# Adding up the squares of an rms norm before the matrix of ones: fewer one-column products, more adds on GpSimd and VectorE

## The chip, the cores and the metric

The kernel runs on one core of one Trainium2 chip. Its engines are named as the profile names them: PE (TensorE products), PEld (TensorE weight loads), DVE (VectorE), ACT (ScalarE), POOL (GpSimd) and SP (SyncE, which issues the transfers). The metric is the device time of one execution, in microseconds; less is better.

## The reference, cut to what matters

The reference is a transformer of two parts in float32, for 256 tokens of 1024 features. Everything that the change touches is the rms norm over the features:

```
def rms_norm(x, g):
    xf = x.astype(F32)
    y = xf * lax.rsqrt(jnp.mean(xf * xf, axis=-1, keepdims=True) + EPS)
    return (y * g.astype(F32)).astype(x.dtype)

# first part: two layers
x = x + diff_attention_mixer(rms_norm(x, ...), mem, ...)      # layer A; the memory is normed too
x = x + dense_swiglu(rms_norm(x, ...), ...)
x = x + hgrn2_mixer(rms_norm(x, ...), mem, ...)               # layer B
x = x + moe_swiglu(rms_norm(x, ...), ...)                     # 8 experts, 2 for each token
x = rms_norm(x, final_norm)
# second part: twice
a = rms_norm_2(h, pre_mix_g[i])
mix = ... attention and gating of a ... @ w_o[i]
h = h + rms_norm_2(mix, post_mix_g[i])
f = conv_ffn(rms_norm_2(h, pre_ffn_g[i]), ...)
h = h + rms_norm_2(f, post_ffn_g[i])
gate = sigmoid(rms_norm_2(h, ple_norm_g[i]) @ w_ple_gate[i])
h = h + gate * (p[i] @ w_ple_proj[i])
```

That makes sixteen norms over 1024 features in one execution.

## The kernel before, in words

Activations are kept transposed: features on the 128 partitions, tokens along the free dimension. x is `xr`, eight blocks of 128 features by 256 tokens; `xpair(i)` is two such blocks side by side, 128x512. Products go into PSUM tiles of 128x512; each float32 operand is split into a rounded high part and a rest, and a product is made of three (`mm3`, L258 to L260, operands by features; `mm3t`, L264 to L266, by tokens). Weights are loaded by SP in pieces of 1 MB and split by ACT (L229, high part) and DVE (L230, rest).

A norm is never applied to the operand: the products are made with x itself, and what comes out is multiplied by 1/rms. So the work of a norm runs beside the products that need it. It has these steps.

1. `squares` (L333 to L340): ACT squares the four pairs of x into four tiles `sq` of 128x512 (L334). With `how="later"` POOL adds the second to the first and the fourth to the third (L337), and two tiles are left. Otherwise DVE adds the second and the third to the first (L339), and the first and the fourth are left.
2. `stats_r` (L342 to L355): PE sums over the partitions, by products that have a 128x128 block of `sq` as weights and the column `onec` (all 1/1024) as the moving operand (L350). The two tiles make eight such products into `ms`, one column for each 128 tokens; each stands in the trace as two records. DVE adds EPS (L353, tile `s`), POOL takes the power -1/2 (L354, tile `r`).
3. `rows_R` (L357 to L366): PE transposes `r` into `R`, 1/rms along the free dimension (L361), and DVE copies it to SBUF in most places (L365).

Eleven norms are of the kind "later": those of layer A and of its memory, of the dense block, of layer B, of the mixture of experts, and in each of the two rounds of the second part one before the mixer, one before the feed-forward block and one before the gate. Five are of the other kinds: `final_norm` (how="now") and the four in `post` (how="acc"), which norm a sum `acc` that lies in PSUM after its last product. In these five everything that follows needs the result: the products of the next block have the normed x as operand. `fill` gives PE part of another product there (`proj`, tiles `pj`); by the numbers in FILL it does so in `final_norm` and in the two `post` of the second round, and not in the two `post` of the first.

The code writes a norm ahead of the products of its block. Where its instructions stand on each engine is settled when the program is built: they are placed among the instructions that are written behind them, and from then on each engine takes its instructions in that order. PE's order is what matters below: a product on `sq` that is not ready holds up all products behind it.

Of the kernel before, what the change touches and what calls it, by code (L numbers as in the profile page):

```python
# [15 lines left out]
OP = mybir.AluOpType  # L16
# [77 lines left out]

# vectors over the features, as columns of 128: (key, how many columns)
COLS = [("a_norm_mix", 8), ("a_mem_norm", 8), ("b_mem_norm", 8), ("dense_norm", 8), ("b_norm_mix", 8), ("moe_norm", 8),
# [14 lines left out]
def layout(v):  # L111
    """the arrays of the launch: the weights as they come, the rest laid out as the chip reads it"""
    def feat(a):
        n = a.shape[1] // 128
        return a.T.reshape(n, 128, a.shape[0]).transpose(1, 0, 2)

    arr = {k: v[k] for k in WEIGHTS}
    arr["consts"] = CONSTS
    arr["xt"] = feat(v["x"][0])
    arr["memt"] = feat(v["mem"][0])  # L120
    router = v["moe_router"][0].reshape(8, 128, 8).transpose(1, 0, 2).reshape(128, 64)
    arr["cols"] = np.concatenate([v[k].reshape(n, 128).T for k, n in COLS] + [router], 1)
    arr["cols2"] = np.stack([np.concatenate(
        [v[k][i].reshape(n, 128).T for k, n in COLS_2]
        + [v["cmp_w2_2"][i].reshape(2, 2, 128, 64).transpose(2, 0, 1, 3).reshape(128, 256)], 1) for i in range(2)])
    arr["rows"] = np.concatenate([v[k].reshape(-1) for k, _ in ROWS]
                                 + [v[k][i].reshape(-1) for i in range(2) for k, _ in ROWS_2])
    arr["pt"] = np.stack([feat(v["p_2"][i, 0]) for i in range(2)])
    arr["wst"] = v["gmlp_ws_2"].transpose(0, 3, 1, 2).reshape(2, 128, 1024)
    return {k: np.ascontiguousarray(a) for k, a in arr.items()}  # L130
# [3 lines left out]
def body(ctx: ExitStack, tc: tile.TileContext, I, out, stop=None):  # L134
# [53 lines left out]
    def C(n, dt=F32):  # L188
        """n columns that stay"""
        o = used[dt]  # L190
        used[dt] += n
        assert used[dt] <= keep[dt].shape[1]
        return keep[dt][:, o:o + n]
# [52 lines left out]
    def wpieces(w, k0, kn, c0, width, s):  # L246
        """wtile in pieces of 512, which leaves its tiles to what is under way"""
        wh, wl = Pieces(), Pieces()
        for k in range(kn):
            for f in range(width // 512):  # L250
                st, hi, lo = G("st" + s), G2("hi" + s, F32R), G("lo" + s, F32R)
                nc.sync.dma_start(st, w[(k0 + k) * 128:(k0 + k) * 128 + 128, c0 + f * 512:c0 + f * 512 + 512])
                split(st, hi, lo, None)
                wh.tiles[k, f], wl.tiles[k, f] = hi, lo
        return wh, wl
# [67 lines left out]
    def sumsq(dst, src, n, eng):  # L323
# [3 lines left out]
        else:  # L327
            V.scalar_tensor_tensor(j[:, :n], src, 1.0 / n, src, op0=OP.mult, op1=OP.mult, accum_out=dst)

    def squares(src, how):  # L330
        """tiles whose sum over features, through the matrix of ones, is the mean square"""
        sq = [J("sq") for _ in range(4)]
        for i in range(4):  # L333
            A.activation(sq[i], src(i), AF.Square)  # L334
            if how == "later":
                if i % 2:
                    GP.tensor_tensor(sq[i - 1], sq[i - 1], sq[i], op=OP.add)  # L337
            elif i in (1, 2):
                V.tensor_tensor(sq[0], sq[0], sq[i], op=OP.add)  # L339
        return sq[0:3:2] if how == "later" else sq[0:4:3]  # L340

    def stats_r(src, how="later"):  # L342
        """1 / rms over the 1024 features, by token"""
        tiles = squares(src, how)
        ps = PC("ms")
        for n, t in enumerate(tiles):
            for c in range(2):
                for kk in range(2):
                    o = kk * 256 + c * 128
                    T.matmul(ps[:, c:c + 1], lhsT=t[:, o:o + 128], rhs=onec, start=n == 0 and c == 0 and kk == 0,  # L350
                             stop=n == len(tiles) - 1 and kk == 1, skip_group_check=True)
        r, m = S(2, "r"), S(2)
        V.tensor_scalar(m, ps[:, 0:2], EPS, None, op0=OP.add)  # L353
        GP.tensor_tensor(r, m, neghalf[:, :2], op=OP.pow)  # L354
        return r  # L355

    def rows_R(r, keep=True):  # L357
        """the same along the free dimension"""
        pr = PC("R")
        for c in range(2):  # L360
            T.transpose(pr[:, c * 128:c * 128 + 128], r[:, c:c + 1].to_broadcast([128, 128]), ident)  # L361
        if not keep:
            return pr[:, :256]
        R = G("R")
        V.tensor_copy(R[:, :256], pr[:, :256])  # L365
        return R[:, :256]  # L366
# [40 lines left out]
    def feat_1024(X, w, s, order, side=None, hook=None):  # L407
        """X times w, by features; side yields what it makes of X while the rest is multiplied"""
        acc = acc_open()
        for n, kp in enumerate(order):  # L410
            if side is not None and n == len(order) - 1:
                steps(side)
            wh, wl = wtile(w, kp * 2, 2, 0, 1024, s)
            acc_rows(acc, wh, wl, [(X.hi(k), X.lo(k)) for k in (kp * 2, kp * 2 + 1)], n == 0, n == len(order) - 1,
                     side)
            if side is not None:
                steps(side, 1)
            if hook is not None and n == 1:
                hook()
        return acc  # L420
# [39 lines left out]

# [1 line left out]
    opening = wload(I["a_w_in"][0], 0, 8, 0, 256, "q")  # L462
# [5 lines left out]

# [1 line left out]
    def mem_load():  # L470
# [5 lines left out]
    def steps(gen, n=None):  # L476
        """runs n steps of a generator (all of them without n); whether it goes on"""
        while n is None or n > 0:
            if next(gen, 0) == 0:
                return False  # L480
            n = None if n is None else n - 1
        return True
# [37 lines left out]
    def by_R(lst, R, f=None, tile=G):  # L520
        """keeps a product by features, times R"""
        def done(ps):
# [8 lines left out]
    def by_r(lst, r, func=AF.Copy, tile=G):  # L531
        """keeps a product by tokens, times r"""
        def done(ps):
            g = tile("tk")
            for c in range(2):
                A.activation(g[:, c * 256:c * 256 + 256], ps[:, c * 256:c * 256 + 256], func, scale=r[:, c:c + 1])
            lst.append(g)
        return done
# [6 lines left out]
    def mem_attn(qmT, kmT, vm, XC):  # L545
        """attention over the memory (queries scaled), its output in pair 3 of XC"""
        cc = G("ccm")
# [43 lines left out]
    def head_rms(po, extra, XC, hp, col):  # L591
        """rms norm of two heads by token and (times extra), then their transposes, split"""
        sq = J("sq")
# [70 lines left out]

# [1 line left out]
    def layer_a():  # L666
# [115 lines left out]

# [1 line left out]
    def layer_b(kv_b, X, r, R):  # L784
# [204 lines left out]

# [1 line left out]
    def moe(acc):  # L991
        # the first weights, before the branch
        ahead = []
# [20 lines left out]
        for k in range(8):  # L1014
            for c in range(2):
                T.matmul(pl[:, c * 8:c * 8 + 8], lhsT=xr[:, k, c * 128:c * 128 + 128], rhs=wr[:, k * 8:k * 8 + 8],
                         start=k == 0 and c == 0, stop=k == 7, skip_group_check=True)
        # tokens by rows, split
        xh = [[G("xh", F32R) for _ in range(2)] for _ in range(2)]
# [45 lines left out]

        # the rms of the tokens, and the weights of their two experts
        r = stats_r(xpair)
# [147 lines left out]

# [1 line left out]
    shared, names = {}, {}  # L1217

    def prep_half(X, k, cols):
        """the operand of feature block k of x"""  # L1220
        if k % 2 == 0:
# [4 lines left out]
    def post(acc, gain, cols, fill):  # L1226
        """adds the normalized acc; the operand of the next products comes with it"""
        r = stats_r(lambda i: acc[i], "acc")
# [17 lines left out]
    def proj(i, out):  # L1246
        """p @ w_ple_proj, features by rows, halved (the gate's own half lies in tanh)"""
        for m in range(2):
# [18 lines left out]
    def gelu_gen(x, n):  # L1267
        """x (1 + tanh(...)) in place: twice the gelu"""
        sq, t = G2("gs"), G2("gt")
# [21 lines left out]
    def second(i, pj, fill, X):  # L1291
# [116 lines left out]

        # keys and values
        seg1 = []  # L1410
# [12 lines left out]
        steps(ex, PRE[0])  # L1423
        # queries, their two parts side by side
        qhl = []
# [144 lines left out]
        def cmp_attn(c):  # L1570
            """over the compressed keys: opens at[c]"""
            ps = PC("cs")
# [265 lines left out]
```

## Time and profile before

| | |
|---|---|
| time, median of 3 runs | 2308.17 us (2307.86 to 2312.56) |
| span of the profiled execution | 2313.2 us |
| PE busy | 2239.2 us (97%) |
| DVE, ACT busy | 1817.8 us (79%), 1474.7 us (64%) |
| POOL busy | 76.4 us (3%) |
| mean granted TensorE clock | 0.977 |

The profiled execution's own time is not listed apart from its span; the span stands 0.6 us above the highest of the three runs and 5.0 us above their median. The experts take about 1000 us in the middle of the span; no norm lies in them. The granted clock is 1.00 (2.4 GHz) or 0.50 (1.2 GHz).

### The profile page before, as it was taken

What the parts mean: (1) busy time and instruction counts of PE and PEld (TensorE: products, weight loads), DVE (VectorE), ACT (ScalarE), POOL (GpSimd) and SP (SyncE); (2) the same over time, 40 slices, a digit from 0 to 9 for tenths busy, and PEclk for the clock granted to TensorE, in tenths of its full rate; (3) what the DMA queues carried; (4) which work ended last, traced back from release to release, by engine and by line L of the source; (5) the groups of instructions that cost most, each with busy time, mean ns of one, the idle gap of its engine ahead of it and who ended that gap; (6) DMA issues with size and microseconds to landing.
All of it is one profiled execution on the core that took longest, in us unless ns stands there. A gap on an engine that the chain in (4) does not pass through costs nothing. (4 is left out here: it accounts for less than half of the span.)

```text
span 2313.2 us, 36939 instructions
## 1 busy us (share of the span) xinstructions
PE 2239.2 (97%) x14218; PEld 2019.2 (87%) x14218; DVE 1817.8 (79%) x2701; ACT 1474.7 (64%) x2138; POOL 76.4 (3%) x83
## 2 busy tenths in 40 slices
PE   8999999998999999999999999999999999989998
PEld 7889999997878888888888888879899998989998
DVE  6666576766888898989898989888777777867776
ACT  5554457435777777777777777777665565765554
POOL 0100001000000000000000000000000001000001
PEclk9999999998999999999999999999999999989998
DMA  8445556224999999999999999986245544525550
GB/s 288 139 137 174 195 171 204 92 78 167 359 348 335 349 353 372 338 354 351 373 350 341 349 378 350 372 299 221 74 136 193 182 147 137 186 78 183 183 178 19
DMA packets 297113, 551.23 MB, mean 238 GB/s; under 512 B 10336, under 2 KB 132064, under 8 KB 296928
## 3 DMA queue, kind: packets, MB, share of 16 engines
q1 hardware_dynamic: 296928, 548.78, 67.5%
q8 instruction: 114, 1.87, 0.3%
q14 instruction: 71, 0.58, 0.1%
HBM read 547.70 MB, written 1.05 MB: 237 GB/s over the span
## 5 line engine op out<-in xcount | busy, mean ns | idle before, releaser
L230 DVE TENSOR_TENSOR loe<-ste,hie 128x1024 fp32r<-128x1024 f32 x448 | 520.0, 1217 | 12.4 <-ACT hie L229 4.2
L229 ACT ACTIVATE hie<-ste 128x1024 fp32r<-128x1024 f32 x448 | 439.5, 1053 | 23.9 <-PE ac L260 9.9
L230 DVE TENSOR_TENSOR lod<-std,hid 128x1024 fp32r<-128x1024 f32 x224 | 264.9, 1218 | 17.1 <-ACT hid L229 15.6
L229 ACT ACTIVATE hid<-std 128x1024 fp32r<-128x1024 f32 x224 | 221.4, 1057 | 4.8 <-PE pg L265 2.3
L266 PE MATMUL pu<-loe,eh 128*128 128x512 f32 x448 | 176.7, 394 | 1.4 <-DVE loe L230 1.4
L1159 PE MATMUL y<-hid,hl 128*128 128x512 f32 x448 | 175.7, 392 | 2.0 <-DVE hl L284 2.0
L264 PE MATMUL pg<-hie,eh 128*128 128x512 f32 x448 | 175.4, 391 | 0.3 <-ACT eh L286 0.3
L266 PE MATMUL pg<-loe,eh 128*128 128x512 f32 x448 | 175.6, 392 | 0.0
L264 PE MATMUL pu<-hie,eh 128*128 128x512 f32 x448 | 174.7, 390 | 0.0
L265 PE MATMUL pg<-hie,el 128*128 128x512 f32 x448 | 174.6, 390 | 0.0
L265 PE MATMUL pu<-hie,el 128*128 128x512 f32 x448 | 174.6, 390 | 0.0
L1158 PE MATMUL y<-hid,hh 128*128 128x512 f32 x448 | 173.4, 392 | 0.7 <-ACT hh L283 0.7
L1137 ACT ACTIVATE eh<-pg,cw 128x512 f32<-128x512 f32 x56 | 38.6, 689 | 203.4 <-PE pg L266 203.4
L1160 PE MATMUL y<-lod,hh 128*128 128x512 f32 x448 | 163.4, 407 | 0.8
L258 PE MATMUL gu<-xh,hig 128*128 128x256 f32 x528 | 150.8, 286 | 3.7 <-ACT xh L286 3.7
L230 DVE TENSOR_TENSOR lou<-stu,hiu 128x1024 fp32r<-128x1024 f32 x66 | 80.4, 1220 | 91.1 <-PE gu L259 82.9
L259 PE MATMUL gu<-xh,log 128*128 128x256 f32 x528 | 150.5, 285 | 0.0
L260 PE MATMUL gu<-xl,hiu 128*128 128x256 f32 x528 | 150.5, 285 | 0.0
L258 PE MATMUL gu<-xh,hiu 128*128 128x256 f32 x528 | 150.4, 285 | 0.0
L259 PE MATMUL gu<-xh,lou 128*128 128x256 f32 x528 | 150.3, 285 | 0.0
L260 PE MATMUL gu<-xl,hig 128*128 128x256 f32 x528 | 150.1, 285 | 0.0
L258 PE MATMUL ac<-hh,hidn 128*128 128x256 f32 x528 | 149.4, 283 | 0.0
(516 smaller groups left out, 6279.5 us busy)
## 6 DMA issues: line engine op xcount, KB each, us to landing
ste<-in_moe_w_gate_up_dram SPq DMA_DIRECT2D x224, 1024.0 KB, 7.2
std<-in_moe_w_down_dram SPq DMA_DIRECT2D x112, 1024.0 KB, 5.5
stg<-in_w_up_dram SPq DMA_DIRECT2D x22, 1024.0 KB, 5.1
stu<-in_w_up_dram SPq DMA_DIRECT2D x22, 1024.0 KB, 5.1
stdn<-in_w_down_dram SPq DMA_DIRECT2D x22, 1024.0 KB, 4.8
stg<-in_dense_w_gate_up_dram SPq DMA_DIRECT2D x11, 1024.0 KB, 5.0
stu<-in_dense_w_gate_up_dram SPq DMA_DIRECT2D x11, 1024.0 KB, 5.0
stdn<-in_dense_w_down_dram SPq DMA_DIRECT2D x11, 1024.0 KB, 4.9
```

The lines of the kernel that those rows point to most:

```text
L229: A.activation(hi[:, :m], sq, AF.Copy)
L230: V.tensor_tensor(lo[:, :m], sq, hi.bitcast(F32)[:, :m], op=OP.subtract)
L258: T.matmul(o, lhsT=lh, rhs=rh, start=start, stop=False, **kw)
L259: T.matmul(o, lhsT=ll, rhs=rh, start=False, stop=False, **kw)
L260: T.matmul(o, lhsT=lh, rhs=rl, start=False, stop=stop, **kw)
L264: T.matmul(o, lhsT=xh, rhs=wh, start=start, stop=False, **kw)
L265: T.matmul(o, lhsT=xl, rhs=wh, start=False, stop=False, **kw)
L266: T.matmul(o, lhsT=xh, rhs=wl, start=False, stop=stop, **kw)
L1137: A.activation(t, pg, AF.Silu, scale=rc)
L1158: T.matmul(y[hf], lhsT=h[:, fs], rhs=a, start=opens, stop=False)
L1159: T.matmul(y[hf], lhsT=l[:, fs], rhs=a, start=False, stop=False)
L1160: T.matmul(y[hf], lhsT=h[:, fs], rhs=b, start=False, stop=ends)
```

## The change

The squares are added up further before PE sees them. With "later", POOL adds the second remaining tile to the first (128x512), and then the right half of that tile to its left half (128x256, the new function `halves`); one tile of 128x256 is left, and two products instead of eight. In the five other norms ACT squares the fourth pair in two halves, DVE adds the right half of the summed tile to its left half and the left half of the fourth pair's squares to that, and two tiles of 128x256 are left: four products instead of eight. Removed comments and text strings are left out of the diff.

```
+    def halves(t):
+        GP.tensor_tensor(t[:, :256], t[:, :256], t[:, 256:], op=OP.add)
+        return t[:, :256]
+
     def squares(src, how):
         sq = [J("sq") for _ in range(4)]
-        for i in range(4):
-            A.activation(sq[i], src(i), AF.Square)
-            if how == "later":
+        if how == "later":
+            for i in range(4):
+                A.activation(sq[i], src(i), AF.Square)
                 if i % 2:
                     GP.tensor_tensor(sq[i - 1], sq[i - 1], sq[i], op=OP.add)
-            elif i in (1, 2):
+            GP.tensor_tensor(sq[0], sq[0], sq[2], op=OP.add)
+            return [halves(sq[0])]
+        for i in range(3):
+            A.activation(sq[i], src(i), AF.Square)
+            if i:
                 V.tensor_tensor(sq[0], sq[0], sq[i], op=OP.add)
-        return sq[0:3:2] if how == "later" else sq[0:4:3]
+        for kk in range(2):
+            A.activation(sq[3][:, kk * 256:kk * 256 + 256], src(3)[:, kk * 256:kk * 256 + 256], AF.Square)
+        V.tensor_tensor(sq[0][:, :256], sq[0][:, :256], sq[0][:, 256:], op=OP.add)
+        V.tensor_tensor(sq[0][:, :256], sq[0][:, :256], sq[3][:, :256], op=OP.add)
+        return [sq[0][:, :256], sq[3][:, 256:]]

     def stats_r(src, how="later"):
         tiles = squares(src, how)
         ps = PC("ms")
         for n, t in enumerate(tiles):
             for c in range(2):
-                for kk in range(2):
-                    o = kk * 256 + c * 128
-                    T.matmul(ps[:, c:c + 1], lhsT=t[:, o:o + 128], rhs=onec, start=n == 0 and c == 0 and kk == 0,
-                             stop=n == len(tiles) - 1 and kk == 1, skip_group_check=True)
+                T.matmul(ps[:, c:c + 1], lhsT=t[:, c * 128:c * 128 + 128], rhs=onec, start=n == 0 and c == 0,
+                         stop=n == len(tiles) - 1, skip_group_check=True)
```

The lines behind it move down by eleven: the products `ms` are L361 after the change, the transposes L372.

**DVE in the `post` behind the first feed-forward block of the second part.** Before the change, from the two adds of squares (L339) to the step that adds EPS (L353); `lopg` are rests of the next block's weights:

```order
L339 TENSOR_TENSOR sq_32288<-sq_32288,sq_32289 128x512
L339 TENSOR_TENSOR sq_32288<-sq_32288,sq_32290 128x512
L230 TENSOR_TENSOR lopg_32525<-stpg_32522,hipg_32524 128x1024
L230 TENSOR_TENSOR lopg_32529<-stpg_32522,hipg_32528 128x1024
L353 TENSOR_SCALAR s_32308<-ms_32298 128x2
L1241 TENSOR_TENSOR pt_32311<-pt_32311,R_32323 128x256 x2
L1242 TENSOR_TENSOR keep<-keep,pt_32311 128x256 x2
```

After the change (the two new adds are L351 and L352):

```order
L348 TENSOR_TENSOR sq_32258<-sq_32258,sq_32259 128x512
L348 TENSOR_TENSOR sq_32258<-sq_32258,sq_32260 128x512
L230 TENSOR_TENSOR lopg_32490<-stpg_32487,hipg_32489 128x1024
L351 TENSOR_TENSOR sq_32258<-sq_32258 128x256
L230 TENSOR_TENSOR lopg_32494<-stpg_32487,hipg_32493 128x1024
L352 TENSOR_TENSOR sq_32258<-sq_32258,sq_32261 128x256
L364 TENSOR_SCALAR s_32277<-ms_32271 128x2
L1252 TENSOR_TENSOR pt_32280<-pt_32280,R_32292 128x256 x2
```

One split of weights now stands between the second add and the first new one, and another between the two new ones. The same holds in the three other `post`; in `final_norm` two splits and a split of `proj` stand there.

**PE in the norm ahead of the first feed-forward block of the second part.** Before the change, around its second group of `ms` and its transposes `R`; `gu` are the block's products:

```order
L258 MATMUL gu_30062<-xh_30004,hig_30046 128x256
L350 MATMUL ms_30022<-keep,sq_30014 128x1 x4
L259 MATMUL gu_30062<-xh_30004,log_30047 128x256
L260 MATMUL gu_30062<-xl_30005,hig_30046 128x256
L258 MATMUL gu_30063<-xh_30004,hig_30046 128x256
L259 MATMUL gu_30063<-xh_30004,log_30047 128x256
L260 MATMUL gu_30063<-xl_30005,hig_30046 128x256
L258 MATMUL gu_30062<-xh_30004,hiu_30056 128x256
L259 MATMUL gu_30062<-xh_30004,lou_30057 128x256
L361 MATMUL R_30035<-keep,r_30031 128x128 x2
L260 MATMUL gu_30062<-xl_30005,hiu_30056 128x256
```

After the change:

```order
L258 MATMUL gu_30033<-xh_29978,hig_30016 128x256
L259 MATMUL gu_30033<-xh_29978,log_30017 128x256
L361 MATMUL ms_29998<-keep,sq_29986 128x1 x2
L260 MATMUL gu_30033<-xl_29979,hig_30016 128x256
L258 MATMUL gu_30032<-xh_29978,hiu_30026 128x256
L259 MATMUL gu_30032<-xh_29978,lou_30027 128x256
L260 MATMUL gu_30032<-xl_29979,hiu_30026 128x256
L372 MATMUL R_30005<-keep,r_30001 128x128 x2
L258 MATMUL gu_30033<-xh_29978,hiu_30026 128x256
L259 MATMUL gu_30033<-xh_29978,lou_30027 128x256
L260 MATMUL gu_30033<-xl_29979,hiu_30026 128x256
```

The first group of `ms`, 41 products ahead, is gone; the one that is left stands seven products later among the `gu` than the second group did, and `R` four products later than before.

**PE in the first norm of the second round of the second part.** Before the change, from the second group of `ms` on; `tw` are products by tokens, 128x512:

```order
L264 MATMUL tw_32704<-hiz_8382_32741,xh_32662 128x512
L265 MATMUL tw_32704<-hiz_8382_32741,xl_32663 128x512
L266 MATMUL tw_32704<-loz_8383_32742,xh_32662 128x512
L350 MATMUL ms_32686<-keep,sq_32678 128x1 x4
L264 MATMUL tw_32703<-hiz_8382_32741,xh_32662 128x512
L265 MATMUL tw_32703<-hiz_8382_32741,xl_32663 128x512
L266 MATMUL tw_32703<-loz_8383_32742,xh_32662 128x512
L264 MATMUL tw_32704<-hiz_8382_32741,xh_32662 128x512
L265 MATMUL tw_32704<-hiz_8382_32741,xl_32663 128x512
```

After the change:

```order
L266 MATMUL tw_32664<-loz_8383_32703,xh_32627 128x512
L264 MATMUL tw_32665<-hiz_8382_32702,xh_32627 128x512
L361 MATMUL ms_32653<-keep,sq_32641 128x1 x2
L265 MATMUL tw_32665<-hiz_8382_32702,xl_32628 128x512
L266 MATMUL tw_32665<-loz_8383_32703,xh_32627 128x512
L264 MATMUL tw_32664<-hiz_8384_32706,xh_32633 128x512
L265 MATMUL tw_32664<-hiz_8384_32706,xl_32634 128x512
L266 MATMUL tw_32664<-loz_8385_32707,xh_32633 128x512
```

The first group, fifteen products ahead, is gone, and the group that is left stands four products later than the second group did.

## Rows read from the trace of the kernel before

**Rows 1.** The page: busy time, share of the span and instructions of each engine

```profile
PE 2239.2 (97%) x14218; PEld 2019.2 (87%) x14218; DVE 1817.8 (79%) x2701; ACT 1474.7 (64%) x2138; POOL 76.4 (3%) x83
```

**Rows 2.** Waits of PE: waiting line, what ended it; us in total, times, longest

```profile
PE R L361 <- POOL r L354: 8.4, 8, 1.3
...
PE ms L350 <- POOL sq L337: 4.4, 5, 1.8
```

**Rows 3.** Instructions on tile sq: count, then shortest/median/longest ns, first and last start

```profile
L350 PE MATMUL ms<-keep,sq x256: 164/250/352, 13.5 to 2290.1; 128*128 128x1 f32 x128
...
L337 POOL TENSOR_TENSOR sq<-sq,sq x22: 1273/1408/2463, 11.1 to 2286.3; 128x512 f32<-128x512 f32 x22
```

**Rows 4.** Groups by line and shape, POOL: count, busy us, mean ns, idle before

```profile
L337 POOL TENSOR_TENSOR sq<-sq,sq 128x512 f32<-128x512 f32 x22 | 36.1, 1643 | 327.9 <-ACT sq L334 291.0 <-PE ac L260 13.6 <-issue 10.7
```

**Rows 5.** Timeline, post behind the first feed-forward block: start us, us

```profile
1890.07 0.69 DVE L339 TENSOR_TENSOR sq<-sq,sq 128x512 f32<-128x512 f32 x1 [0.32 <-ACT sq L334]
...
1890.68 2.35 DVE L230 TENSOR_TENSOR lopg<-stpg,hipg 128x1024 fp32r<-128x1024 f32 x2
...
1890.91 1.92 PE L350 MATMUL ms<-keep,sq 128*128 128x1 f32 x16 [0.43 <-DVE sq L339]
...
1892.95 0.15 DVE L353 TENSOR_SCALAR s<-ms 128x2 f32<-128x2 f32 x1
...
1893.93 0.43 PE L361 MATMUL R<-keep,r 128*128 128x128 f32 x2 [1.11 <-POOL r L354]
...
1896.15 0.58 PE L258 MATMUL fp<-xh,hipg 128*128 128x256 f32 x1 [1.79 <-ACT xh L286]
```

**Rows 6.** Groups by line and shape, DVE: an add of 128x256 in SBUF

```profile
L651 DVE TENSOR_TENSOR cv<-cv 128x256 f32<-128x256 f32 x44 | 18.4, 421 | 0.0
```

**Rows 7.** Timeline, norm ahead of the second part's first feed-forward block

```profile
1705.14 2.13 POOL L337 TENSOR_TENSOR sq<-sq,sq 128x512 f32<-128x512 f32 x1 [6.36 <-ACT sq L334]
...
1707.33 1.05 PE L350 MATMUL ms<-keep,sq 128*128 128x1 f32 x8 [0.62 <-POOL sq L337]
...
1709.42 0.43 PE L361 MATMUL R<-keep,r 128*128 128x128 f32 x2
```

**Rows 8.** Timelines of POOL and of PE, norm of layer B

```profile
346.23 3.91 POOL L337 TENSOR_TENSOR sq<-sq,sq 128x512 f32<-128x512 f32 x2 [191.07 <-ACT sq L334]
...
353.12 1.84 PE L350 MATMUL ms<-keep,sq 128*128 128x1 f32 x16
...
357.57 0.43 PE L361 MATMUL R<-keep,r 128*128 128x128 f32 x2 [1.07 <-POOL r L354]
```

**Rows 9.** Timeline, first norm of the second part's second round

```profile
1929.22 2.34 POOL L337 TENSOR_TENSOR sq<-sq,sq 128x512 f32<-128x512 f32 x1 [17.96 <-ACT sq L334]
...
1930.35 1.75 DVE L1748 TENSOR_TENSOR keep<-keep,sg 128x512 f32<-128x512 f32 x1
...
1931.61 1.49 PE L350 MATMUL ms<-keep,sq 128*128 128x1 f32 x8 [1.76 <-POOL sq L337]
...
1933.90 1.27 POOL L337 TENSOR_TENSOR sq<-sq,sq 128x512 f32<-128x512 f32 x1 [2.35 <-ACT sq L334]
...
1939.22 0.95 PE L350 MATMUL ms<-keep,sq 128*128 128x1 f32 x8
```

**Rows 10.** Timeline of POOL: second add in the first and the last norm

```profile
14.68 1.28 POOL L337 TENSOR_TENSOR sq<-sq,sq 128x512 f32<-128x512 f32 x1 [2.27 <-ACT sq L334]
...
2286.26 2.22 POOL L337 TENSOR_TENSOR sq<-sq,sq 128x512 f32<-128x512 f32 x1 [3.68 <-issue]
```

**Rows 11.** Stretches: length, busy us (instructions) by engine, granted clock, DMA

```profile
147.90:155.60 7.70, 5.66 (x46) 5.46 (x47) 5.67 (x8) 3.89 (x7) 3.98 (x3) 1.00 0.00 0
1894.50:1901.30 6.80, 5.15 (x24) 5.15 (x25) 6.80 (x17) 4.58 (x10) 1.34 (x1) 0.50 0.45 150
1932.10:1938.90 6.80, 6.80 (x20) 5.54 (x20) 2.11 (x4) 2.59 (x4) 1.27 (x1) 0.50 0.23 81
...
68.40:78.60 10.20, 9.31 (x44) 9.02 (x44) 3.63 (x5) 2.66 (x4) 2.59 (x2) 0.50 0.35 119
```

## The prediction, made before the changed kernel was run

> **What bounds the kernel now.** I read the page first: PE is busy 97% of the span [rows 1]. So PE is the bound nearly everywhere, and PE work that goes away is worth its full time, unless PE then only comes earlier to a wait. Next the waits of PE: two of the longest kinds lie inside the norms, 8.4 us before the transposes `R` (for POOL's power) and 4.4 us before products `ms` (for POOL's adds) [rows 2]. PE takes its products in order, so each of these stops everything behind it. Then the instructions on `sq`: 256 records of `ms`, that is 128 products in two records each, and 22 adds on POOL of 1273 to 2463 ns [rows 3], mean 1643 [rows 4]. Last the timelines of the sixteen norms, for who waits for whom in each; four of them stand in rows.
>
> **What is removed.** Sixteen records in the norm of layer B take 1.84 us from the first start to the last end [rows 8], or about 0.12 us a record when they come one behind the other. Eleven norms lose 12 records and five lose 8: 172 records, 20.6 us of PE. That is the most that the change can give by itself; what it puts in the place of the products decides.
>
> **Five norms on the path (`final_norm`, `post`).** In the `post` behind the first feed-forward block the second add of squares ends at 1890.76, and PE then has nothing but the 16 records, 1890.91 to 1892.83; the step `s` follows at 1892.95, `R` at 1893.93, and the first product of the next block at 1896.15, after 1.79 us more of idling [rows 5]. POOL is not in this chain ahead of the power. After the change DVE's order is: second add, split, add, split, add. A split is half of 2.35 us, 1.17 [rows 5]; an add of 128x256 in SBUF takes 0.42 [rows 6]. That is 2 x 1.17 + 2 x 0.42 = 3.18 us from 1890.76, to 1893.95. Only then come the products, in PE's order all eight records behind the last add: 8 x 0.12, and `s` at 1895.0 instead of 1892.95. **+2.05 us**; nothing covers it, since PE has no other work there. The other `post` of that round, by the same rows of its own, gives +1.75. In the second round PE has products `pj` meanwhile, which now run ahead of `ms`, so that only +0.45 and +0.8 are left (there `s` follows the same 3.2 us after the second add). In `final_norm` a split of `proj` stands in DVE's order too, but most of `pj` is still to be done: +1.0. Together **+6.0 us**. The squares in two halves on ACT cost nothing: both are done while DVE is in the splits.
>
> **The eleven others: a longer chain on POOL.** Two adds more stand between POOL's second add and `ms`. The 128x512 one: 1.27 at best, 2.46 at worst, 1.64 in the mean [rows 3, 4]; I take the mean, since these are the same operands on the same engine beside the same work. The 128x256 one no row shows; it has half of the elements, so between half of the shortest and half of the longest whole add, 0.64 to 1.23; I take 0.7. The chain is 2.34 us longer, between 1.91 and 3.69.
> A rule of the Trainium skill (GPSIMD Engine Reference, section 4.1, Engine selection) speaks against this: adds of two tensors belong on VectorE, GpSimd being about two times slower. The same shape takes 0.69 on DVE [rows 5] and 1.64 on POOL [rows 4], 2.4 times. With the page's factor the chain would be 2.1 longer, not 2.34, and the sum below 2.1 us smaller, 2314.8; I go by the row.
>
> For each norm I take PE's place in the new order (so many products behind the old place, at 0.12 us for one of 256 columns, 0.23 for one of 512), without the first group of `ms` and the wait before it; compare it with POOL's new end; and count the products that now stand ahead of `R` as done.
> - Layer B: POOL's second add ends at 350.14, 3 us before PE comes to `ms`, which stands where it stood; two adds more still fit in. 12 records less, `R` waits for the power as before, all of it earlier: **-1.9** [rows 8].
> - Ahead of the second part's first feed-forward block: POOL's second add ends at 1707.27, and PE already waited 0.62 for it [rows 7]. POOL is now done at 1709.7; PE, without the first group and seven products on, is there at 1706.6 and waits 3.1 us. Then half a microsecond of `ms`, `s` and the power; `R` comes at 1711.3 instead of 1709.42, with four products (0.5 us) more behind it: **+1.4**.
> - First norm of the second round: the first group, its wait of 1.76 and the 1.49 that it took are gone. The second add ends at 1935.17, the chain at 1937.55; PE is there at 1934.2 (19 products of 0.23 from 1929.85, where its old wait began) and waits 3.4. Against 1940.2 before, with four products more done: **-3.1** [rows 9].
> - The norm of the experts gives 0: there the products wait for DVE's choice of experts, not for the norm.
> - The other seven by the same working, the first and the last of them with their second add in [rows 10]: -2.1, -2.1, 0, -0.2, +1.5, +0.7, -0.2, together -2.4.
>
> Sum **-6.1 us**; with a chain of 1.91 it would be -9.5, with 3.69 it would be +6.6.
>
> **What the new waits do to the clock.** PE's waits of about 2.5 to 3.5 us before `ms` are new in four places: the dense block's norm, those ahead of both feed-forward blocks of the second part, and the one with the -3.1. In the trace the stretch around the dense norm, which holds the longest of the old waits before `R`, 1.3 us, has a granted clock of 1.00 [rows 2, 11]. Behind the wait of 1.76 us it is 0.50, the level of 1.2 GHz, for 6.8 us [rows 9, 11], and so it is behind the `post` with its waits of 1.11 and 1.79 [rows 5, 11]. While PE has work, half of such a stretch is lost: 3.4 us for 6.8. Not all of it is work, and some stretches are shorter; I take 2.2 for each, 4 x 2.2 = **+8.8 us** (from 0, if the clock stays, to 4 x 3.4 = 13.6).
>
> **Sum.** 6.0 - 6.1 + 8.8 = +8.7 us. The profiled execution would go from a span of 2313.2 to 2321.9. That span lies 5.0 us above the median of the runs, 0.2%; I add the same 8.7 to the median: **2316.9 us**.
>
> **Rivals.**
> 1. *The clock does not fall at the new waits.* For it speaks that the stretch around the dense norm held 1.00 with two waits in it [rows 11]; against it, that the waits are now twice as long. The sum is 6.0 - 6.1 = -0.1: 2308.1, no change. Chance 0.22.
> 2. *Faster: the first groups no longer break the stream.* Around the memory's norm in layer A the clock is 0.50 for 10.2 us [rows 11], behind a first group that PE had to wait for. That group goes. If the clock stays at 1.00 over the new wait there (1.2 to 1.6 us), as it does around the dense norm with 1.3, 5.1 us come back; that is the point from which it decides. With POOL's shortest adds and no new falls as in 1, the sum is 6.0 - 9.5 - 5.1 = -8.6: 2299.6. Against it: POOL's adds rarely run at their shortest beside DVE's splits. Chance 0.12.
> 3. *Slower still: POOL holds DVE.* While POOL added for 2.34 us, an add on DVE of 128x512 took 1.75 instead of 0.69 [rows 5, 9]: 1.06 us lost. The change has 22 adds more on POOL. In most places splits lie ahead in stock and cover it; if half of the 22 hold a split or an operand that PE is about to need, 11 x 1.06 = 11.7 us come on top: 2328.6. Chance 0.14.
> The same page of the Trainium skill (section 1, Specifications) says that GpSimd shares its SBUF interfaces with VectorE, which contend where an instruction reads two inputs from SBUF; by that rule 3 has its mechanism, and the trace agrees with the 1.75.
>
> **How the numbers follow.** The forecast has 0.52, its own range 2312 to 2322 (the chain from 1.91 to 2.8, each fall of the clock 1.5 to 3 us). A measurement of this kernel can tell about 0.2%, 4.6 us, from no change: 2303.6 to 2312.8. Slower: 0.52 + 0.14, less 0.04 of the forecast that ends under 2312.8: 0.62. Same: 0.22 + 0.04. Faster: 0.12. To hold the time 8 times in 10 the range takes in rival 1 and the lower part of rival 3: 2303.5 to 2325.
>
> **What the profile would show.** Right: 84 instead of 256 records of `ms`; in the four `post` DVE's last add about 3.2 us behind the second; PE waits of 2 to 3.5 us before `ms` that end with POOL's add of 128x256; new stretches at 0.50 behind them, above all ahead of both feed-forward blocks. Wrong: POOL's two new adds together under 2 us, `ms` without waits, or the clock at 1.00 after them (rival 1); DVE's adds and splits above their old durations while POOL adds (rival 3). The prediction would fall most likely by the clock, the term least supported by rows.

## The result, and the profile of the changed kernel

The changed kernel takes 2329.28 us (median of 4 runs, 2322.25 to 2332.60), the kernel before in the same sitting 2308.02 (2306.85 to 2312.56). The two medians lie 21.3 us apart; the ratio on record over all runs is 1.0079 with a 95% interval of 1.0063 to 1.0095, which is 18.2 us more on 2308.0, and this is the number used below. Forecast were 8.7 more, 2316.9, and at most 2325. The side was right, the size less than half.

The page, part 1, in the profiled execution (2330.53 us, span 2328.7):

```profile
PE 2227.5 (96%) x14046; PEld 2005.6 (86%) x14046; DVE 1831.5 (79%) x2711; ACT 1476.0 (63%) x2143; POOL 100.6 (4%) x105
```

Beside [rows 1] the 172 records are gone and PE is busy 11.7 us less, but the span is 15.5 us longer: PE stands idle 27.2 us more. The waits of PE that have to do with norms say where (waiting line, what ended it; us in total, times, longest):

```profile
PE ms L361 <- POOL sq L332: 24.3, 11, 3.8
...
PE R L372 <- POOL r L365: 10.9, 9, 2.4
...
PE ms L361 <- DVE sq L352: 6.9, 3, 3.4
```

All eleven norms that add on POOL (the later norms from here on) now make PE wait for the fold, 24.3 us against 4.4 in five places before [rows 2]. Three of the other five wait 6.9 us for VectorE's last add. The adds themselves, from the instructions on `sq` (count, shortest/median/longest ns) and the groups by line on POOL (busy us, mean ns):

```profile
L361 PE MATMUL ms<-keep,sq x84: 169/250/374, 18.5 to 2305.5; 128*128 128x1 f32 x84
...
L343 POOL TENSOR_TENSOR sq<-sq,sq x11: 1261/1322/1366, 16.3 to 2302.7; 128x512 f32<-128x512 f32 x11
L332 POOL TENSOR_TENSOR sq<-sq x11: 726/732/1593, 17.7 to 2304.1; 128x256 f32<-128x256 f32 x11
```
```profile
L342 POOL TENSOR_TENSOR sq<-sq,sq 128x512 f32<-128x512 f32 x22 | 36.7, 1670 | 321.3 <-ACT sq L340 284.6 <-PE ac L260 13.6 <-DVE xl L287 12.3
...
L343 POOL TENSOR_TENSOR sq<-sq,sq 128x512 f32<-128x512 f32 x11 | 14.4, 1313 | 0.9
L332 POOL TENSOR_TENSOR sq<-sq 128x256 f32<-128x256 f32 x11 | 10.7, 974 | 0.9
```

Third add and fold take 1.31 + 0.97 = 2.29 us in the mean; the forecast had 1.64 + 0.70 = 2.34. The chain is as long as forecast, by two errors that cancel. What it did to the clock, in stretches behind the norms (the column after POOL's count is the granted clock):

```profile
150.40:158.10 7.70, 5.14 (x31) 5.08 (x31) 6.41 (x7) 2.56 (x3) 3.12 (x4) 0.78 0.36 122
354.90:365.10 10.20, 7.79 (x42) 7.50 (x42) 6.50 (x9) 1.77 (x3) 1.62 (x1) 0.67 1.00 311
...
1716.80:1723.60 6.80, 6.73 (x30) 6.46 (x31) 2.77 (x5) 1.81 (x2) 0.72 (x2) 0.50 0.18 63
1904.50:1914.70 10.20, 6.95 (x30) 6.49 (x31) 6.55 (x20) 5.69 (x12) 0.97 (x2) 0.50 0.33 104
1952.30:1955.70 3.40, 3.40 (x10) 2.73 (x10) 1.52 (x4) 1.06 (x1) 0.80 (x2) 0.50 0.01 2
2303.90:2310.70 6.80, 4.95 (x22) 4.66 (x23) 2.41 (x4) 0.63 (x1) 2.45 (x3) 0.50 0.00 0
```

The dense norm (first row), at 1.00 before [rows 11], has fallen to 0.50 for part of its stretch. So has layer B's (second row), where the forecast saw no wait at all. The `post` behind the first feed-forward block is at 0.50 for 10.2 us instead of 6.8. The first norm of the second round (the row at 1952.30), at 0.50 for 6.8 us before [rows 11], is there for 3.4.

At ScalarE's first square of a norm, the changed kernel is 0.9 us ahead in the dense norm, then behind: 5.8 us at the experts' norm, 7.0 at the first `post`, 13.2 at the norm ahead of the gate in the first round, 14.0 in the last. One step lies around the dense and layer B norms, one around the two `post` of the first round and the norms behind them.

Layer B's norm shows both ways in which POOL's chain tells (start us, us):

```profile
347.03 4.25 POOL L342 TENSOR_TENSOR sq<-sq,sq 128x512 f32<-128x512 f32 x2 [192.12 <-ACT sq L340]
...
351.36 1.37 POOL L343 TENSOR_TENSOR sq<-sq,sq 128x512 f32<-128x512 f32 x1
351.48 2.32 DVE L230 TENSOR_TENSOR lofz<-stfz,hifz 128x1024 fp32r<-128x1024 f32 x1
352.80 1.59 POOL L332 TENSOR_TENSOR sq<-sq 128x256 f32<-128x256 f32 x1
353.73 1.34 DVE L287 SCALAR_TENSOR_TENSOR xl<-keep,xh 128x256 fp32r<-128x256 f32 x2
...
354.45 0.67 PE L361 MATMUL ms<-keep,sq 128*128 128x1 f32 x4 [1.57 <-POOL sq L332]
354.99 3.48 DVE L230 TENSOR_TENSOR lofz<-stfz,hifz 128x1024 fp32r<-128x1024 f32 x3
358.39 0.15 DVE L364 TENSOR_SCALAR s<-ms 128x2 f32<-128x2 f32 x1
358.46 1.21 DVE L230 TENSOR_TENSOR lofz<-stfz,hifz 128x1024 fp32r<-128x1024 f32 x1
358.62 1.62 POOL L365 TENSOR_TENSOR r<-s,keep 128x2 f32<-128x2 f32 x1 [4.23 <-DVE s L364]
...
360.30 0.43 PE L372 MATMUL R<-keep,r 128*128 128x128 f32 x2 [2.41 <-POOL r L365]
```

PE waits 1.57 us for the fold. And POOL and VectorE hold each other up. The split that starts 0.12 us behind POOL's third add takes 2.32 us, where the three at 354.99, with POOL idle, take 3.48 together. The fold starts while that split runs and takes 1.59 us; the split at 358.46 starts ahead of POOL's power and takes its usual 1.21, and the power takes 1.62 us. The products are done at 355.12, but `s` has to stand behind three more splits, until 358.39, and `R` waits 2.41 us where it waited 1.07 [rows 8]. Before the change `s` stood behind three splits as well, but these came 2.7 us earlier:

```profile
352.27 3.48 DVE L230 TENSOR_TENSOR lofz<-stfz,hifz 128x1024 fp32r<-128x1024 f32 x3
355.67 0.14 DVE L353 TENSOR_SCALAR s<-ms 128x2 f32<-128x2 f32 x1
```

### The profile page after: what moved, and what is told of

Its sections match the earlier page's. It is cut to its first block, busy times and chain, and to the rows that moved or that the text cites. A ratio compares the mean times of both kernels' runs of the same rounds, so it can differ in the third digit from the quotient of the medians.

```text
span 2328.7 us, 36637 instructions
## 1 busy us (share of the span) xinstructions
PE 2227.5 (96%) x14046; PEld 2005.6 (86%) x14046; DVE 1831.5 (79%) x2711; ACT 1476.0 (63%) x2143; POOL 100.6 (4%) x105
## 3 DMA queue, kind: packets, MB, share of 16 engines
q8 instruction: 112, 1.84, 0.3%
HBM read 547.70 MB, written 1.05 MB: 236 GB/s over the span
```

## The experiments

Each kernel ran beside the kernel before; the last column works the ratio out on 2308.0 us. "At 0.50" is 2 x (1 - mean granted clock) x span, in the mean over the runs: the time at the lower of the two levels that the stretches show. The kernel before has 90 to 98 us of it in the sittings.

| run | ratio, 95% interval | at 0.50, us | us |
|---|---|---|---|
| changed kernel | 1.0079 (1.0063 to 1.0095) | 128 | +18.2 |
| e1 POOL's part alone | 1.0066 (1.0053 to 1.0079) | 117 | +15.2 |
| e2 VectorE's part alone | 1.0021 (1.0010 to 1.0032) | 102 | +4.8 |
| e3 POOL's part without the fold | 1.0042 (1.0029 to 1.0055) | 109 | +9.7 |
| e4 later norms added on VectorE | 0.9872 (0.9856 to 0.9887) | 74 | -29.5 |
| e5 as e1, `ms` further back | 0.9984 (0.9975 to 0.9993) | 95 | -3.7 |
| e6 before, its pairs on VectorE | 0.9917 (0.9904 to 0.9930) | 79 | -19.2 |
| e7 before, two idle adds more on POOL | 1.0042 (1.0028 to 1.0057) | 98 | +9.7 |
| e8 before, `ms` further back | 0.9929 (0.9916 to 0.9943) | 78 | -16.4 |
| e9 changed, waits fed | 1.0054 (1.0041 to 1.0067) | 90 | +12.5 |
| e10 as e2, adds ahead of the splits | 0.9995 (0.9986 to 1.0004) | 91 | -1.2 |
| e11 e4 and e10 | 0.9871 (0.9856 to 0.9885) | 79 | -29.8 |
| e12 as e4 without the fold | 0.9880 (0.9867 to 0.9894) | 70 | -27.7 |
| e13 changed kernel again | 1.0078 (1.0065 to 1.0091) | 130 | +18.0 |
| e14 changed, waits fed to fit | 1.0054 (1.0039 to 1.0069) | 101 | +12.5 |
| e15 as e7, behind the power | 1.0024 (1.0015 to 1.0033) | 95 | +5.5 |

**Which part costs (e1 to e4).** e1 keeps the old code of the five other norms, e2 that of the later norms. e3 is e1 with:

```diff
-            return [halves(sq[0])]
+            return [sq[0]]
```

and e4 is e1 with all adds of the later norms on VectorE:

```diff
             for i in range(4):
                 A.activation(sq[i], src(i), AF.Square)
-                if i % 2:
-                    GP.tensor_tensor(sq[i - 1], sq[i - 1], sq[i], op=OP.add)
-            GP.tensor_tensor(sq[0], sq[0], sq[2], op=OP.add)
-            return [halves(sq[0])]
+                if i:
+                    V.tensor_tensor(sq[0], sq[0], sq[i], op=OP.add)
+            V.tensor_tensor(sq[0][:, :256], sq[0][:, :256], sq[0][:, 256:], op=OP.add)
+            return [sq[0][:, :256]]
```

Expected of e1: 

> Only the eleven later norms are changed (third add and fold on GpSimd, 4 records); final_norm and the four post stay as before. My theory now, by the offsets between the two traces: these norms carry about 9 of the 15.5 us by which the profiled span grew, through waits of PE before ms that end with POOL's fold and through the clock behind them: 2315 to 2320 us, ratio 1.003 to 1.005. Rival, the forecast's own terms (first groups of products gone, -6.1; clock +8.8): +2.7, 2311 us. Rival, only the five norms on the path cost: 2302 to 2308.

Expected of e2: 

> Only final_norm and the four post are changed (squares of half tiles, fold and third add on VectorE, 8 records); the eleven later norms stay as before. By the working of the forecast and by the offsets of the trace after: +6 to +6.5, 2314 to 2315 us, ratio 1.0026 to 1.0028; with a fall of the clock behind the two long waits of PE up to +9. Rival, these norms carry nearly the whole loss: 2321 to 2327.

Expected of e3: 

> The later norms with POOL's third add of 128x512 but without the fold: 4 products in 8 records from one tile; the other five norms as before. The chain on POOL is 0.7 to 1.6 us shorter than in the run with the fold, and PE has 4 records more. If the length of the chain decides (each microsecond is waited for by PE): about 5 us under the run with the fold and its waits before ms shorter by 0.7 to 1.6. If every new wait costs alike because the clock falls behind it, whatever its length: within 2 us of the run with the fold.

Expected of e4: 

> The later norms with all four adds on VectorE (three of 128x512, one fold of 128x256, as each square comes), none on GpSimd; 4 records; the other five norms as before. Theory that GpSimd's slow adds, and what they hold up on VectorE, are the loss: sums are ready some 4 us earlier, no waits of PE before ms, 2300 to 2306 us. Rival, VectorE is full around the norms (83% busy over the span) and 2.5 us of adds in each of 11 norms push splits back that PE needs: 2312 to 2325 us, with PE waiting for xl and lo instead.

The parts add up, 15.2 + 4.8 = 20.0 against 18.2, and POOL's part carries three quarters; e1 lies above its expected 1.003 to 1.005. e3 bears out the length of the chain: 5.5 us come back with the fold gone. e4 ended far below every expectation of mine (the 83% in its text is a slip; VectorE is 79% busy in both kernels): the same 4 records in each norm, the same number of adds, and 45 us less than e1. Its waits:

```profile
PE R L371 <- POOL r L364: 6.6, 8, 1.2
...
PE ms L360 <- DVE s L1056: 3.0, 1, 3.0
...
PE ms L360 <- DVE sq L348: 2.7, 2, 2.2
...
PE ms L360 <- DVE sq L343: 1.2, 1, 1.2
```

PE waits before `ms` of a later norm in two places, 4.2 us in all, against 24.2 in e1. But two things differ from e1, not one: who adds, and where `ms` stands. Where VectorE makes the adds, the order that is settled when the program is built has `ms` further back. Products that stand ahead of `ms` in PE's order, from the start of the program, those of `ms` and `R` not counted (the second group, in the kernel before):

| norm | before | changed | e4 | e5 |
|---|---|---|---|---|
| layer A, memory | 373 | 381 | 412 | 417 |
| dense | 912 | 919 | 944 | 943 |
| ahead of the first feed-forward block, second part | 13735 | 13742 | 13768 | 13768 |
| the same, second round | 16330 | 16335 | 16364 | 16366 |
| the last | 17936 | 17950 | 17969 | 17966 |

**Place or engine (e5 to e8).** e5 is e1, and e8 the kernel before, with the products of `ms` traced at a lower priority, one number for each later norm, which moves them to where e4 has them in eight of the eleven (not in the first norm, layer B's and the experts'):

```diff
+    LATE = [400, 132, 74, 0, 0, 78, 154, 95, 86, 152, 126]
...
+        with tc.high_priority(-LATE.pop(0) if how == "later" else 0):
```

e6 is the kernel before with `V.tensor_tensor` for `GP.tensor_tensor` in the two adds. e7 is the kernel before with, in each later norm, an add of 128x512 and one of 128x256 more on POOL, on squares that nobody reads any more.

Expected of e5: 

> As the run of GpSimd's part alone (its chain of four adds, 4 records in each later norm), but the products ms stand further back in TensorE's order in eight of the eleven norms: 10 to 40 products later, where they stand when VectorE makes the adds. Theory of the place: the loss came from products that stood too early for GpSimd's chain; with 1.2 to 4 us of other products ahead of them PE no longer waits, about 19 us of idling and the clock behind it come back and most of the way to the run with VectorE's adds is made: 2285 to 2300 us. Rival, the engine: GpSimd's adds hold VectorE's splits up by about 10 us more than before, wherever ms stands, and the wait goes to xl, lo or R: 2312 to 2325 us.

Expected of e6: 

> The kernel before with its two adds of each later norm on VectorE instead of GpSimd; 16 records as before, no add more. Theory of the engine (GpSimd's adds are long, vary and hold VectorE): most of the 29 us that VectorE's adds gave come without any record less: 2285 to 2298 us. Theory of the count: the 132 records fewer carry it (15.8 us of PE), so here only some 5 to 10 us: 2299 to 2305. Theory of the place: the second group stands 5 to 11 products further back only, about 5 to 8 us: 2301 to 2306.

Expected of e7: 

> The kernel before, with two adds more on GpSimd in each later norm (128x512 and 128x256, on squares that are no longer needed) behind the power, where nobody waits for them: the price of GpSimd's adds for the work beside them alone. If what they hold up on VectorE (excess over usual durations 10.8 us in the trace before, 20.7 in the changed one) reaches the path: 5 to 12 us more, 2315 to 2322. If VectorE's stock of splits covers it: within 3 us of the kernel before.

Expected of e8: 

> The kernel before (two adds on GpSimd, 16 records), only its products ms stand further back in TensorE's order in the later norms, both groups together where they stand when VectorE makes the adds. Theory of the place: the waits for the first groups (0.99, 0.79 and 1.76 us in the trace before) and the stretches of half clock behind them go: 8 to 18 us less, 2293 to 2303 us. If the place is worth nothing without the fewer records and the free VectorE: 2307 to 2313.

Both theories hold in part: e6 and e7 ended as that of the engine had it, e8 as that of the place, and e5 between the two. The place of `ms` is worth 18.9 us in e5 against e1, and 16.4 in e8 against the kernel before, where nothing else is changed. With `ms` at its new place in both, POOL's longer chain costs 12.7 us (e5 against e8) although it saves 132 records. e5 still waits for the fold in six norms:

```profile
PE ms L363 <- POOL sq L332: 13.1, 6, 3.0
...
PE R L374 <- POOL r L367: 10.6, 7, 3.7
```

e6 gains 19.2 us with 16 records as before, but it does not show the engine alone: in its order the first groups of `ms` stand up to 30 products further back too, and the second up to 11, which its expectation left out for the first. With the place held, e4 against e5 shows the engine: the same four adds and 4 records, `ms` within five products of the same place in ten of the eleven norms, and 25.8 us between them. In e7 two adds that nobody reads cost 9.7 us. They stood ahead of the power in POOL's order in most norms, though, so that I tried them again behind it:

```diff
+            for add in (GP.tensor_tensor(a, a, c, op=OP.add),
+                        GP.tensor_tensor(c[:, :256], a[:, :256], a[:, 256:], op=OP.add)):
+                tc.add_manual_dep(add.ins, power.ins.name, ...)
```

Expected: 

> The kernel before with the two extra adds on GpSimd in each later norm strictly behind the power, so that nothing on GpSimd waits for them; TensorE's order is that of the kernel before. What is left of the 9.7 us of the earlier run is VectorE held up alone. If that was the price: 5 to 10 us more than before, 2317 to 2321. If the delay of the power was: within 3 us of the kernel before.

5.5 us remain, between the two expectations. They may be VectorE held up, or tiles of squares that come free later since POOL still reads them; the runs don't separate these.

**VectorE's part (e10 to e12).** In e10 the splits that stood between the adds of the five other norms are ordered behind the last add; e11 puts e10 and e4 together; e12 is e4 without the fold.

Expected of e10: 

> As the run of VectorE's part alone (final_norm and the four post changed), but in each of these five norms the two splits of weights that stood between the second, the third and the fourth add come behind the fourth. The term of the forecast for these norms was 2 x 1.17 us of splits plus two adds of 0.42, less the records that go. If the splits in between are the price: the sum is there 2.3 us earlier in each, the loss of about 5 us goes, 2306 to 2311 us. Rival, the splits are then late themselves by 0.84 us and the next block waits for them, or the two adds and ScalarE's half squares are the price: 2313 to 2317.

Expected of e11: 

> Both that helped or may help: the later norms with all four adds on VectorE and 4 records, and the five other norms changed as in the run with the adds ahead of the splits (8 records). If the parts add up: the 2281 us of the first, changed by what the other run of this call shows against the kernel before, between -3 and +3: 2278 to 2285 us, under both kernels. If VectorE's adds in the one delay the splits of the other: 2285 to 2292.

Expected of e12: 

> The later norms with three adds on VectorE and no fold: 4 products in 8 records, standing 8 to 13 products earlier in TensorE's order than with the fold. Two adds on VectorE with 16 records gave 0.9917 of the time before, four adds with 4 records 0.9872. If the count of records carries that difference, each 44 of them (12 us per 100): 0.988 to 0.990, 2284 to 2288 us. If the place in TensorE's order carries it: nearer to the run with two adds, 2288 to 2292; if the fold on VectorE costs more than its 4 records: 2277 to 2281.

e10: the loss of e2 is gone, so the splits in between were its price. The same place, the `post` behind the first feed-forward block, in the changed kernel and then in e10 (timelines of DVE and PE):

```profile
1901.15 0.69 DVE L348 TENSOR_TENSOR sq<-sq,sq 128x512 f32<-128x512 f32 x1 [0.32 <-ACT sq L346]
...
1902.90 0.42 DVE L351 TENSOR_TENSOR sq<-sq 128x256 f32<-128x256 f32 x1
1903.23 1.22 DVE L230 TENSOR_TENSOR lopg<-stpg,hipg 128x1024 fp32r<-128x1024 f32 x1
1904.37 0.42 DVE L352 TENSOR_TENSOR sq<-sq,sq 128x256 f32<-128x256 f32 x1
...
1904.93 1.84 PE L361 MATMUL ms<-keep,sq 128*128 128x1 f32 x8 [3.37 <-DVE sq L352]
...
1906.81 0.16 DVE L364 TENSOR_SCALAR s<-ms 128x2 f32<-128x2 f32 x1 [2.02 <-PE ms L361]
```
```profile
1890.38 0.69 DVE L353 TENSOR_TENSOR sq<-sq,sq 128x512 f32<-128x512 f32 x1 [0.32 <-ACT sq L351]
1891.11 0.42 DVE L356 TENSOR_TENSOR sq<-sq 128x256 f32<-128x256 f32 x1
1891.83 0.43 DVE L357 TENSOR_TENSOR sq<-sq,sq 128x256 f32<-128x256 f32 x1 [0.30 <-ACT sq L355]
...
1892.40 1.02 PE L370 MATMUL ms<-keep,sq 128*128 128x1 f32 x8 [1.62 <-DVE sq L357]
...
1893.46 0.16 DVE L373 TENSOR_SCALAR s<-ms 128x2 f32<-128x2 f32 x1
```

From the second add to `s` it is 5.66 us in the one, 3.08 in the other. But 8 records fewer bring nothing either: e10 is no faster than the kernel before, and e11 no faster than e4. e12 against e6 and e4: going from 16 records to 8 on VectorE gives 8.5 us, from 8 to 4 another 1.8, less than the intervals can tell; in both steps `ms` moves back as well, so that these are no prices of the records alone.

**The clock (e9, e13, e14).** In the changed kernel, products of 128x256 whose result is not used stand right ahead of `ms` in each later norm, on squares that are ready after POOL's second add: four in e9, one to three in e14, by the wait. They fill the wait with work; `ms` itself stands within seven products of its place in the changed kernel.

Expected of e9: 

> The changed kernel with four products of 128x256 more in each later norm, right ahead of ms in TensorE's order (on squares that are there after GpSimd's second add; their result is not used). They run in the wait for the third add and the fold and bring ms no earlier. Over the runs so far the mean granted clock gives about 92 us of half clock before and 128 after, and the span without half of that is the same in both, 2263 us. Theory that the clock is the loss: the falls go although the chain is as long, half clock back to 95 to 110 us, 2312 to 2321 us. Rival, the waits themselves are the loss: 2328 to 2334 us, the feeding products costing a little more where a wait is short.

Expected of e13: 

> The changed kernel once more, on the chip of the two other runs of this call: 1.0063 to 1.0095 of the time before, half clock by the mean granted clock of the runs 120 to 136 us.

Expected of e14: 

> The changed kernel with one to three feeding products in each later norm instead of four, as many as its wait before ms holds by the trace of the changed kernel. If the clock makes 12 to 18 of the 18 us: half clock near 90 to 100 us as with four, less delay of R, 2312 to 2319 us. If the falls cost little and the waits are the loss: half clock may rise again, 2322 to 2330 us.

The time at 0.50 falls from 130 us (e13) to 101 (e14) and 90 (e9, the level of the kernel before), with a chain on POOL as long as ever. The total gains 5.5 us by the ratios of e13 and e14 (7.5 by their medians, 2328.14 and 2320.67), and the intervals just touch: e9, 2320.5 by its ratio, lies at the upper edge of what the theory of the clock expected, and e14, with the same total, between its two theories. The feeding products are in the way themselves: e14's 27 are 54 records, and PE now waits longer for `R`.

```profile
PE R L388 <- POOL r L381: 14.8, 13, 4.0
...
PE ms L374 <- POOL sq L332: 5.7, 8, 1.3
```

So the falls do come from PE's idling before `ms`, and 5.5 us is the least that they seem to cost. How much they cost in all I can only estimate. In the 68 runs of the kernel before in the four sittings of the experiments, the time at 0.50 goes from 78 to 106 us, and the span rises 0.36 us for each of it; where PE works all through, it would be half a microsecond, since 0.50 is half of 1.00. The 36 to 39 us more of the changed kernel are then 13 to 20 us. The slope need not be the clock's alone: longer waits in a run would raise both.

## Why the prediction was too low

- *172 records, 20.6 us*: the count is right, 84 are left. That they are worth 0.12 us each on the path no run shows: from e6 to e4 132 of them go for 10.3 us, with two more adds on VectorE and `ms` further back, and in e10 the 40 of the other five norms bring no gain clear of the noise.
- *Five norms on the path, +6.0*: right. e2 gives 4.8 (2.3 to 7.4), and e10 shows that the two splits in between are the price. In the `post` worked out in the prediction, VectorE's last add ends 2.95 us behind the second (3.18 forecast); `s` is then 0.7 us later than reckoned, because the 8 records took 1.84 us at the lower clock instead of 0.96.
- *POOL's chain, 2.34 us longer*: right in the mean, 2.29, but by luck. The mean of the rows was too long for the third add (1.64 against 1.31), and 0.7, a little over half of the shortest whole add, too short for the fold (0.97); three folds took 1.59, above the 1.23 that was to be the longest.
- *Eleven later norms, -6.1*: wrong. This is one of the two steps that failed. (Its terms add up to -6.0.) The working had long new waits before `ms` in four places and let both adds fit ahead of PE in layer B's norm, for -1.9; the trace has a wait for the fold in each of the eleven, 0.6 to 3.8 us, 24.3 together. Two waits that it worked out came near: 2.30 us for 3.1, and 3.56 for 3.4. In layer B POOL's second add ended 1.1 us later than in the rows, the two new adds took 3.1 us instead of 2.34, to 354.39, and PE was there at 352.9; with `R` so late, that norm lost where it should have won. What takes the place of the -6.1 is about zero or a loss (below).
- *What POOL does to VectorE*: priced as rival 3 at 11.7 us with a chance of 0.14, and left out of the sum. It should have been a term, not a rival: it does not exclude the others. Two more adds a norm that nobody reads cost 5.5 to 9.7 us (e15, e7), and in layer B the way is in the rows. The Trainium skill (GPSIMD Engine Reference, section 1, Specifications) has GpSimd's SBUF interfaces shared with VectorE, with contention where a VectorE instruction has two inputs in SBUF. The trace agrees, with 2.32 us for a split that starts behind POOL's add, and 3.48 for three without. The hold goes both ways, which rival 3 left out: where a split has started first, it is POOL's instruction that is long (last section).
- *Clock, +8.8 (0 to 13.6)*: the other step that failed, in size. New falls were forecast in four places. The dense norm and the one ahead of the first feed-forward block of the second part have theirs; the one ahead of the second such block, where PE waits only 1.05 us, has none, and the first norm of the second round had its fall before the change already [rows 11]. Others came where none was reckoned with (layer B's norm, the last one). POOL's part alone has 25 us more at 0.50 than the kernel before, the whole change 36 to 39: an estimated 13 to 20 us where 8.8 stood. The step itself, a price for each fall that is seen coming, was too small because every one of the eleven norms had a wait.

Together: +4.8 for the five norms and +15.2 for the eleven, where +6.0 and +2.7 were forecast. Within the 15.2 the clock's 25 us at 0.50 make 9 to 12.5 by the same estimate, and the rest, 2.7 to 6, is what the new waits and POOL's hold leave over when the records saved are taken off. A finer division stays open: e15 and e14 change more than the one thing that each was made for.

The prediction weighed the Trainium skill's rule that adds of two tensors belong on VectorE (GPSIMD Engine Reference, section 4.1, Engine selection), but used it only to price the adds. Taken at its word it was the way to the faster kernel: e4 makes the same adds on VectorE and is 1.28% under the kernel before. VectorE, at 79% busy, had room for them: of PE's waits before `ms` only the 1.2 us in layer B's norm and the 3.0 in the experts' end with VectorE there.

## What to carry to other kernels

Where an in-order engine waits for a short side chain, look at three things apart: how long the chain is, which engine runs it, and where the waiting instruction stands in its engine's order. Here the engine was worth 26 us with the place held (e5 to e4), the place 16 to 19 with the engine held (e8, e5), and the work saved, which the change was about, some 10 at most (e6 to e4). A side effect on another engine (a slower neighbour, a clock that falls behind each wait) belongs into the sum with a price, not among the rivals, as soon as one row of the trace shows it.

## What the hardware showed unexpectedly

- One and the same program has between 78 and 106 us at the lower clock from run to run, and its time goes with it (correlation 0.83 over 68 runs). The stretch at 0.50 around the memory's norm of layer A [rows 11], on which rival 2 was built, is not a property of the kernel: in e2, whose change begins only at `final_norm`, the profiled execution has 1.00 in its place. The profiled execution of the kernel before, from which the falls were priced, was itself at the upper end, with a mean granted clock of 0.977 where the 68 runs have 0.977 to 0.983.

```profile
62.00:76.00 14.00, 11.62 (x98) 11.21 (x97) 9.14 (x19) 6.94 (x14) 4.71 (x3) 1.00 0.58 191
```

- POOL's fold of 128x256 takes either 0.73 to 0.80 or 1.59 us, and its power on 128x2 either 0.70 to 0.71 or 1.54 to 1.62, in the same kernel on the same shapes. The trace of the changed kernel shows what goes with it: the three long folds and the six long powers all start while a split of weights runs on VectorE, and end 0.55 to 0.59 us after it; the short ones start while none does. So these are waits, as with the split of 2.32 us beside the third add, and whichever of the two engines came second had to wait.
- An add of 128x512 on VectorE takes 0.68 to 0.69 us in all 33 places of e4, where POOL makes none of the adds of squares.
